# Four w_in blocks in whole float32, sums issued ahead, and powers by doubling in a one-core hybrid layer

## The chip, the cores and the metric

The kernel runs on one core of a Trainium2 chip. Its engines are TensorE (PE, and PEld for its weight loads), VectorE (DVE), ScalarE (ACT), GpSimd (POOL) and SyncE (SP, which issues most loads). The metric is device time of one execution in microseconds.

## The reference, cut to what matters

One layer of a hybrid block for 256 tokens of width 1024: a state space mixer and a sparse attention side by side, then a mixture of 32 experts.

```python
mod = cs @ ada_w[l] + ada_b[l]                      # cs = silu(c); six vectors of 1024
sh1, sc1, g1, sh2, sc2, g2 = jnp.split(mod[:, None, :], 6, axis=-1)
h = rms_norm(x, norm1_g[l]) * (1.0 + sc1) + sh1
proj = h @ w_in                                     # q, six k/v blocks, gates, u, merge gates
# s5_mixer(u): powers of ab = exp(lam * dt), complex, 64 states in each of 32 groups
mag = jnp.exp(lr * dt)
ab_re, ab_im = mag * jnp.cos(li * dt), mag * jnp.sin(li * dt)
bu = einsum(ug, bb); s = associative_scan(combine, (a, bu)); y = einsum(s, c) + d_skip * ug
# compress_kv: overlapping blocks of 32 keys (values), each through a small MLP
blocks = kv[:, idx] + pos[:, None, :]
return jax.nn.gelu(blocks @ w1) @ w2
...
merged = g_attn * (attn @ nsa_w_o) + g_ssm * (ssm @ ssm_w_o)
x = x + g1 * (merged @ w_out)
x = x + g2 * hier_moe(rms_norm(x, norm2_g[l]) * (1.0 + sc2) + sh2, ...)
```

## The kernel before, in words

Weights stream from HBM through rings of slots of 8 KB a partition (`room`, `load`, `set_rings`); a load waits until its slot's last reader is done. The first ring has five slots (`ringA`). Loads go out on SP's queue in order.

The first stage computes `mod`, h and the first four blocks of w_in: u0 and u1 (the mixer's input, 256 columns each), kc and vc (keys and values to be compressed). It runs over k = 0 to 7, 128 rows of the model width at a time. For each k:

- `mod_sum` multiplies `csb` (silu of c, repeated) with the part of ada_w for this k in eight float32 matmuls; TensorE packs four of them side by side. ScalarE copies the result to `msk`.
- `mod_end` transposes `msk` on TensorE; DVE reduces it and makes `modT` (shift) and `Gm` (gain).
- DVE makes `hf`, the row block of h, from the normalised and transposed input (`xnT`). ScalarE makes it again, rounded to float32r, as `hTh`; DVE subtracts for the rest, `hTl`.
- ScalarE rounds the slab of w_in for this k to float32r (`hi`, line 381), DVE subtracts for `lo` (line 382). `halves` hands out the two halves of the tiles `whi` and `wlo` in turn.
- `mm3` multiplies: high by high, high by low, low by high, three float32r matmuls of 256 columns each, eight times: 24 for a k.

Later projections (`proj_T`, `proj_N`) go the same way with `split` in place of the slab's halves, and read `hTh` and `hTl` of all k; the first of them is ks.

Beside it DVE and GpSimd prepare the mixer: exponent, sine and cosine of ab in small operations of 16 columns; `pows`, ab to the powers 2 to 4, and `pk4`, multiples of 4 up to 32, each from the one before by `cmul` with six operations; `sq`, two squarings more. GpSimd and DVE multiply B with the powers (`cmul2`), GpSimd C (`cmul`), and DVE copies the C powers to `Vc` (line 579). TensorE transposes the B powers to `Wt`. Then follow U (DVE transposes u), the matmuls x and pst, the projection ks, the compression of the keys (`blk`, `pc`, from line 706), and the scan on GpSimd and DVE. For each of four quarters n a tile `blk` is taken from a pair in turn; GpSimd zeroes its last column, DVE fills the rest.

The order on each engine isn't that of the source: a scheduler with its own estimates sets it when the program is built. Each engine takes its instructions in the order so set.

Of the kernel before, what the change touches and what calls it, by code (L numbers as in the profile page):

```python
# [52 lines left out]
def hybrid(ctx: ExitStack, tc: tile.TileContext, A, out, dbg=None, stop=None):  # L53
# [477 lines left out]
    for j in (2, 3, 4):  # L531
        cmul(V, pows[:, j, 0], pows[:, j, 1], pows[:, j - 1, 0], pows[:, j - 1, 1], pows[:, 1, 0], pows[:, 1, 1], u1, u2)
# [5 lines left out]
    for k in range(2, 9):  # L538
        cmul(V, pk4[:, k, 0], pk4[:, k, 1], pk4[:, k - 1, 0], pk4[:, k - 1, 1], pk4[:, 1, 0], pk4[:, 1, 1], u1, u2)
# [164 lines left out]
    for n in range(4):  # L704
# [4 lines left out]
        blk = cz.tile([128, 2, 4, 4, 16], F32, name=f"blk{n}", tag="blk", bufs=2)  # L709
        G.memset(blk[:, :, :, :, 15:16].rearrange("p k c g o -> p k c (g o)"), 0.0)  # L710
# [717 lines left out]
```

## Time and profile before

| | |
|---|---|
| time, median of 3 runs | 608.26 us (606.21 to 609.49) |
| profiled execution | 604.61 us, span 602.9 us |
| TensorE busy | 532.2 us (88%) |
| weight loads | 364.7 us (60%) |
| DVE busy | 351.0 us (58%) |
| ScalarE busy | 199.1 us (33%) |
| GpSimd busy | 203.2 us (34%) |
| HBM read | 166.30 MB, 278 GB/s over the span |

The shares are means over stages with different limits, so they are read by stage. A row of the timeline gives the start of the first of a run of equal instructions, how long they took together, how many there are, and in brackets the idle time before it with what ended it. Matmuls are pipelined: the distance of their starts tells their rate, not their length. TensorE's granted clock has two levels, 1.2 and 2.4 GHz; 1.00 in a row is the upper one.

### The profile page before, as it was taken

How to read it: one execution, taken by the hardware profiler on the slowest of the kernel's cores; microseconds unless marked ns; L12 is line 12 of the kernel's file. 1: busy time of each engine (PE TensorE's matmuls, PEld its weight loads, DVE VectorE, ACT ScalarE, POOL GpSimd, SP SyncE). 2: the span in 40 equal slices, each digit the busy share in tenths (PEclk: the TensorE clock that was granted, in tenths of full speed). 3: DMA queues.
4: the chain of work that ended last, by engine and by line, in shares of the span. 5: the costliest groups of instructions: out<-in, count | busy, mean ns of one | idle time of the engine just before them, and what ended most of it. 6: DMA issues, size and time to landing. Idle time of an engine off the chain costs nothing. (4 is left out here: it accounts for less than half of the span.)

```text
span 602.9 us, 10837 instructions
## 1 busy us (share of the span) xinstructions
PE 532.2 (88%) x4173; PEld 364.7 (60%) x4174; DVE 351.0 (58%) x942; ACT 199.1 (33%) x461; POOL 203.2 (34%) x299
## 2 busy tenths in 40 slices
PE   0769699879888999999989998999999989999983
PEld 0446597568888888888877997444434433333321
DVE  7999948999477867687866766422222221211213
ACT  3363446332244655554543444111111101010102
POOL 3079307587269544688977000000000000000000
PEclk9999899797998999999999999999999999999997
DMA  8774633967546323654499697977999999999992
GB/s 321 309 270 142 217 133 124 366 202 264 173 179 203 114 106 109 242 167 148 145 382 368 232 403 288 341 278 300 404 422 421 419 419 423 419 421 421 421 366 74
DMA packets 27867, 168.12 MB, mean 279 GB/s; under 512 B 3106, under 2 KB 3234, under 8 KB 10274
## 3 DMA queue, kind: packets, MB, share of 16 engines
q1 hardware_dynamic: 25506, 158.97, 68.4%
q0 software_dynamic: 2304, 8.39, 4.1%
q8 instruction: 35, 0.57, 0.4%
q14 instruction: 22, 0.18, 0.1%
HBM read 166.30 MB, written 1.05 MB: 278 GB/s over the span
## 5 line engine op out<-in xcount | busy, mean ns | idle before, releaser
L1345 POOL TENSOR_TENSOR x<-x,fg 128x512 f32<-128x512 f32 x1 | 1.3, 1269 | 266.4 <-DVE x L1347 266.4
L1188 PE MATMUL guq<-gu,room__4521 128*32 128x512 f32 (+1 forms) x512 | 85.8, 602 | 1.3 <-DMA gu<-in_egu_dram 1.3
L1161 PEld LDWEIGHTS pgq<-room__4521,x 128*128 128x128 f32 x288 | 38.1, 190 | 54.2 <-issue 15.8
L1165 DVE TENSOR_SCALAR room__4521<-pgq,Gm,modT 128x128 f32<-128x128 f32 x36 | 14.7, 409 | 85.0 <-PE pgq L1161 74.4
L1163 ACT ACTIVATE room__4521<-pgq,modT,Gm 128x128 f32<-128x128 f32 x36 | 16.5, 458 | 125.1 <-PE pgq L1161 125.1
L1161 PE MATMUL pgq<-room__4521,x 128*128 128x128 f32 x288 | 50.5, 298 | 7.7 <-DVE room__4521 L1165 4.5
L918 POOL TENSOR_SCALAR pr<-pr,st 128x128 f32<-128x128 f32 (+1 forms) x64 | 38.4, 618 | 26.5 <-DVE st L915 16.4
L353 POOL TENSOR_SCALAR adt<-adt,ct 128x256 f32<-128x256 f32 x64 | 35.4, 570 | 21.5 <-DMA adt<-in_adat_dram 21.4
L240 PE MATMUL pm<-ada,csb 128*32 128x256 f32 x256 | 21.6, 432 | 21.1 <-DVE csb L216 16.6
L1211 PE MATMUL dnq<-ed,acq 128*32 128x512 f32 (+1 forms) x224 | 38.9, 598 | 0.0
L1214 DVE SCALAR_TENSOR_TENSOR gb<-dnq,wsq,gb 128x512 f32<-128x512 f32 x18 | 13.5, 750 | 38.7 <-PE dnq L1211 38.7
L913 ACT ACTIVATE pr<-s,st 128x128 f32<-128x128 f32 (+1 forms) x64 | 26.2, 422 | 27.1 <-DVE st L909 26.3
L1220 PE MATMUL acc<-gb,room__4521 128*128 128x512 f32 x72 | 33.3, 605 | 0.0
L1188 PEld LDWEIGHTS guq<-gu,room__4521 128*32 128x32 f32 (+1 forms) x512 | 16.7, 112 | 24.8 <-issue 16.6
L1220 PEld LDWEIGHTS acc<-gb,room__4521 128*128 128x128 f32 x72 | 12.9, 189 | 20.4 <-issue 20.2
L240 PEld LDWEIGHTS pm<-ada,csb 128*32 128x32 f32 x256 | 7.7, 119 | 28.7 <-DVE csb L216 16.2
L354 POOL TENSOR_TENSOR adt<-adt 128x512 f32<-128x512 f32 x16 | 23.6, 1482 | 0.3
L290 PE MATMUL pj_gs<-hTh,wlo 128*128 128x256 f32 x64 | 19.3, 302 | 2.8 <-DVE wlo L281 2.8
L1211 PEld LDWEIGHTS dnq<-ed,acq 128*32 128x32 f32 (+1 forms) x224 | 9.5, 113 | 19.9 <-issue 17.7
L288 PE MATMUL p<-oTh,whi 128*128 128x256 f32 x64 | 18.4, 287 | 0.8 <-ACT whi L280 0.8
L289 PE MATMUL pj_gs<-hTl,whi 128*128 128x256 f32 x64 | 19.1, 298 | 0.0
L290 PE MATMUL p<-oTh,wlo 128*128 128x256 f32 x64 | 18.4, 288 | 0.6 <-DVE wlo L281 0.6
(558 smaller groups left out, 1600.6 us busy)
## 6 DMA issues: line engine op xcount, KB each, us to landing
gu<-in_egu_dram SPq DMA_DIRECT2D x64, 1024.0 KB, 17.4
ed<-in_edn_dram SPq DMA_DIRECT2D x28, 1024.0 KB, 16.1
ada<-in_adat_dram SPq DMA_DIRECT2D x16, 1024.0 KB, 6.6
adt<-in_adat_dram POOLq DMA_DIRECT2D x16, 512.0 KB, 5.2
slab<-in_w_dram SPq DMA_DIRECT2D x8, 512.0 KB, 8.8
cw<-in_cw_dram SPq DMA_DIRECT2D x4, 1024.0 KB, 4.9
win_q<-in_win_dram SPq DMA_DIRECT2D x4, 1024.0 KB, 4.7
win_gs<-in_win_dram SPq DMA_DIRECT2D x4, 1024.0 KB, 5.7
```

The costliest lines, as they stand in the source:

```text
L240: T.matmul(pm_k[32 * t:32 * t + 32, 0:256], lhsT=csb[:, 2 * t + j], rhs=slot[:, 2 * t + j], start=j == 0, stop=j == 1, tile_position=(0, 3 ...
L288: T.matmul(o, lhsT=ah, rhs=bh, start=start, stop=False)
L289: T.matmul(o, lhsT=ah, rhs=bl, start=False, stop=False)
L290: pe_last[0] = T.matmul(o, lhsT=al, rhs=bh, start=False, stop=stop)
L353: G.tensor_scalar(w[:, t], w[:, t], ct[:, 4 * h + t:4 * h + t + 1], 1.0, op0=ALU.mult, op1=ALU.mult)
L354: G.tensor_add(w[:, 0:2], w[:, 0:2], w[:, 2:4])
L913: S.activation(pr[:, a_:b_], src, AF.Exp, bias=st[:, 1, z:z + 1], scale=0.125, accum_out=st[:, 2, z:z + 1])
L918: G.tensor_scalar(pr[:, a_:b_], pr[:, a_:b_], st[:, 3, z:z + 1], 1.0, op0=ALU.mult, op1=ALU.mult)
L1161: T.matmul(pg[:, k % 4, 0:S_], lhsT=x[:, b, 128 * k:128 * k + 128], rhs=O[:, b, 0:S_], start=b == 0, stop=b == 1)
L1188: gl_ = T.matmul(gu[r], lhsT=xe[:, k, r], rhs=wgu(e, k), start=k == 0, stop=k == 7, tile_position=(0, s_ * e))
L1211: T.matmul(dn[r], lhsT=ac[:, c, r], rhs=wdn(e, c)[:, 512 * h:512 * h + 512], start=c == 0, stop=c == 1, tile_position=(0, s_ * e))
L1220: T.matmul(acc[b][h], lhsT=OT[0:M, sl], rhs=ty2[0:M, h], start=False, stop=last)
```

## The change

- The loop over k multiplies `hf` and the slab as they are, in float32; the slab's `hi` and `lo` are gone. `hTh` is a ScalarE copy of `hf`. A whole-float32 matmul is two instructions on TensorE.
- The sums of two k are issued ahead, and `rows` makes a block's `modT`, `Gm`, `hf` one k ahead of its matmuls; `hf` has three buffers.
- Two slots more for the first loads: the tiles `whi` and `wlo`, not used until ks now.
- The powers come by doubling: `times` multiplies several powers by one in four wider operations.
- ScalarE copies all C powers to `Vc`.
- The key blocks are two fixed tiles, whose last column DVE zeroes once.

```diff
     ada1, slab = [], []
+    set_rings([Late("whi"), Late("wlo")] + [ringA] * NA)
...
+    def rows(p_):
+        mod_end(*p_)
+        k = p_[3]
+        hf = pp.tile([128, 256], F32, name=f"hf{k}", tag="hf", bufs=3)
+        hfs.append(hf)
+        V.tensor_scalar(hf, xnT[:, k], Gm[:, 0, k:k + 1], modT[:, 0, k:k + 1], op0=ALU.mult, op1=ALU.add)
+        S.copy(hTh[:, k], hf)
+        V.tensor_sub(hTl[:, k], hf, f32(hTh[:, k]))
+    pms = [mod_sum(ada1[0], 0, 0, "s"), mod_sum(ada1[1], 0, 1, "s")]
+    rows(pms[0])
     for k in range(8):
-        mod_end(*mod_sum(ada1[k], 0, k, "s"))
-        hf = pp.tile([128, 256], F32, name=f"hf{k}", tag="hf", bufs=2)
...
-        hi, lo = halves()
-        S.copy(hi, slab[k])
-        V.tensor_sub(lo, slab[k], f32(hi))
+        if k < 6:
+            pms.append(mod_sum(ada1[k + 2], 0, k + 2, "s"))
+        if k < 7:
+            rows(pms[k + 1])
+        hf, w4 = hfs[k], slab[k]
         for i in range(2):
             for b in range(2):
-                mm3(o4[i][:, b], hTh[:, k, sl], hTl[:, k, sl], hi[:, c], lo[:, c], k + b == 0, k + b == 8)
+                T.matmul(o4[i][:, b], lhsT=hf[:, 128 * b:128 * b + 128], rhs=w4[:, 256 * i:256 * i + 256], start=k + b == 0, stop=k + b == 8)
...
-    for j in (2, 3, 4):
-        cmul(V, pows[:, j, 0], pows[:, j, 1], pows[:, j - 1, 0], pows[:, j - 1, 1], pows[:, 1, 0], pows[:, 1, 1], u1, u2)
+    def times(o, a, b):
+        n = b.shape[1]
+        p1, p2 = pwt[:, 0, 0:n], pwt[:, 1, 0:n]
+        for p_, r in ((p1, 0), (p2, 1)):
+            V.tensor_tensor(p_, a[:, r].unsqueeze(1).unsqueeze(2).to_broadcast([128, n, 2, 16]), b, op=ALU.mult)
+        V.tensor_sub(o[:, :, 0], p1[:, :, 0], p2[:, :, 1])
+        V.tensor_add(o[:, :, 1], p1[:, :, 1], p2[:, :, 0])
+    times(pows[:, 2:3], pows[:, 1], pows[:, 1:2])
+    times(pows[:, 3:5], pows[:, 2], pows[:, 1:3])
...
-    for k in range(2, 9):
-        cmul(V, pk4[:, k, 0], pk4[:, k, 1], pk4[:, k - 1, 0], pk4[:, k - 1, 1], pk4[:, 1, 0], pk4[:, 1, 1], u1, u2)
+    for n in (1, 2, 4):
+        times(pk4[:, n + 1:2 * n + 1], pk4[:, n], pk4[:, 1:n + 1])
...
-                if j == 0:
-                    S.activation(dst, ccur[r][ps_], AF.Copy, scale=-1.0 if r else 1.0)
-                else:
-                    V.tensor_scalar(dst, ccur[r][ps_], -1.0 if r else 1.0, None, op0=ALU.mult)
+                S.activation(dst, ccur[r][ps_], AF.Copy, scale=-1.0 if r else 1.0)
...
+    blks = [cz.tile([128, 2, 4, 4, 16], F32, name=f"blk{n}") for n in range(2)]
+    for blk in blks:
+        V.memset(blk[:, :, :, :, 15:16].rearrange("p k c g o -> p (k c g o)"), 0.0)
...
-        G.memset(blk[:, :, :, :, 15:16].rearrange("p k c g o -> p k c (g o)"), 0.0)
+        blk = blks[n % 2]
```

The order of the built program shows the moves at three places.

TensorE, from its first sum to its first block. `pm` is the bank of a sum, `msk` its copy, `ph` the transposed xn, `hf` the float32 row block, `hTh` its float32r part. Before:

```order
L240 MATMUL pm_238<-ada_0_85,csb 32x256 x8
L248 MATMUL pm_238<-ident,msk_247 128x128 x2
L229 MATMUL ph_188<-ident,scr 128x128 x4
L229 MATMUL ph_194<-ident,scr 128x128 x4
L229 MATMUL ph_214<-ident,scr 128x128 x4
L229 MATMUL ph_220<-ident,scr 128x128 x4
L288 MATMUL pj_u_234<-whi,hTh 128x256
```

With the change:

```order
L241 MATMUL pm_238<-ada_0_85,csb 32x256 x8
L241 MATMUL pm_249<-ada_1_89,csb 32x256 x8
L249 MATMUL pm_238<-ident,msk_247 128x128 x2
L230 MATMUL ph_188<-ident,scr 128x128 x4
L230 MATMUL ph_194<-ident,scr 128x128 x4
L241 MATMUL pm_270<-ada_2_93,csb 32x256 x8
L249 MATMUL pm_249<-ident,msk_258 128x128 x2
L230 MATMUL ph_214<-ident,scr 128x128 x4
L230 MATMUL ph_220<-ident,scr 128x128 x4
L249 MATMUL pm_270<-ident,msk_279 128x128 x2
L398 MATMUL pj_u_234<-slab_87,hf_266 128x256 x2
```

The sums of k=1 and 2 and their transposes of msk now stand ahead of the first block, whose operands are `hf` and the slab itself.

DVE, between `hf` of k=2 and `hf` of k=3 (here its end). `mr`, `modT`, `Gm` belong to k=3, `pwt`, `pk`, `pwA`, `pwB` to the powers, `scr`, `b` to the B powers. Before, at the same step (`hf` of k=2 is `hf_349`, of k=3 `hf_396`):

```order
L377 TENSOR_SCALAR hf_349<-scr,Gm,modT 128x256
L475 TENSOR_TENSOR u_688<-pows 128x16
L476 TENSOR_TENSOR u_689<-pows 128x16
L251 TENSOR_TENSOR modT<-mr_392,pk 128x2
L467 TENSOR_TENSOR scr<-pows,b_710 128x256
L468 TENSOR_TENSOR scr<-pows,b_709 128x256
L477 TENSOR_TENSOR pows<-u_688,u_689 128x16
L252 SCALAR_TENSOR_TENSOR Gm<-modT,pk 128x1
...
L377 TENSOR_SCALAR hf_396<-scr,Gm,modT 128x256
```

With the change (`hf_345` is that of k=3):

```order
L479 TENSOR_TENSOR scr<-pows,b_565 128x256
L549 TENSOR_TENSOR pwt<-pk_671 128x128
L252 TENSOR_TENSOR modT<-mr_341,pk 128x2
L480 TENSOR_TENSOR b_568<-scr 128x256
L550 TENSOR_TENSOR pk_671<-pwt 128x4x16
L551 TENSOR_TENSOR pk_671<-pwt 128x4x16
L253 SCALAR_TENSOR_TENSOR Gm<-modT,pk 128x1
L478 TENSOR_TENSOR scr<-pows,b_568 128x256
L563 COPY pwA<-pk_671 128x8x16 x2
L564 TENSOR_SCALAR pwB<-pk_671 128x8x16
L383 TENSOR_SCALAR hf_345<-scr,Gm,modT 128x256
```

Before, `hf` of k=3 follows that of k=2 after 11 rows; now nearly all powers stand between the two.

DVE at the last block (k=7). `hf_584` and `hf_450` are its row block before and now; `wlo<-win_ks` are the two low halves of the weights of the next projection. Before:

```order
L377 TENSOR_SCALAR hf_584<-scr,Gm,modT 128x256
L477 TENSOR_TENSOR pk_824<-u_688,u_689 128x16
L379 TENSOR_TENSOR hTl<-hf_584,hTh 128x256
L550 TENSOR_SCALAR aS<-pk_824 128x16
L551 COPY aS<-pk_824 128x16
L472 TENSOR_TENSOR u_688<-pk_824 128x16
...
L551 COPY aS<-sq_887 128x16
L393 STREAM_TRANSPOSE scr<-pj_u_234 128x256 x2
L281 TENSOR_TENSOR wlo<-win_ks,whi 128x1024
L393 STREAM_TRANSPOSE scr<-pj_u_235 128x256 x2
L281 TENSOR_TENSOR wlo<-win_ks,whi 128x1024
```

With the change:

```order
L385 TENSOR_TENSOR hTl<-hf_403,hTh 128x256
L385 TENSOR_TENSOR hTl<-hf_432,hTh 128x256
L282 TENSOR_TENSOR wlo<-win_ks,whi 128x1024
L251 TENSOR_REDUCE mr_446<-pm_415 128x2
L282 TENSOR_TENSOR wlo<-win_ks,whi 128x1024
L252 TENSOR_TENSOR modT<-mr_446,pk 128x2
L253 SCALAR_TENSOR_TENSOR Gm<-modT,pk 128x1
L383 TENSOR_SCALAR hf_450<-scr,Gm,modT 128x256
L385 TENSOR_TENSOR hTl<-hf_450,hTh 128x256
L404 STREAM_TRANSPOSE scr<-pj_u_234 128x256 x2
L404 STREAM_TRANSPOSE scr<-pj_u_235 128x256 x2
```

The two low halves of ks moved from behind the last row block and the transposes of U to in front of them.

## Rows read from the trace of the kernel before

**Rows 1.** Busy time by stretch: us, busy us (instructions) by engine, clock, DMA.
```profile
23.00:81.00 58.00, 45.99 (x357) 35.31 (x355) 56.15 (x206) 26.48 (x53) 31.45 (x38) 0.94 0.56 203
...
30.00:45.00 15.00, 10.25 (x92) 7.56 (x95) 14.86 (x49) 10.09 (x24) 11.50 (x13) 0.93 0.78 274
```
**Rows 2.** Waits, 23 to 81 us: total us, times, longest.
```profile
ACT hTh L378 <- DVE Gm L252: 13.2, 4, 10.2
```
**Rows 3.** DVE's timeline: start, us, engine, line, operation, count [idle before].
```profile
12.46 1.23 DVE L382 TENSOR_TENSOR wlo<-slab,whi 128x1024 fp32r<-128x1024 f32 x1 [0.46 <-ACT whi L381]
...
18.27 1.22 DVE L382 TENSOR_TENSOR wlo<-slab,whi 128x1024 fp32r<-128x1024 f32 x1
...
26.83 0.17 DVE L440 TENSOR_SCALAR r__629<-r__629 128x16 f32<-128x16 f32 x1
...
29.85 0.17 DVE L461 TENSOR_TENSOR pows<-mag,cs__633 128x16 f32<-128x16 f32 x1
```
**Rows 4.** TensorE's timeline, start of the stage, same columns.
```profile
16.57 1.93 PE L240 MATMUL pm<-ada,csb 128*32 128x256 f32 x16 [16.57 <-DVE csb L216]
...
20.49 3.87 PE L229 MATMUL ph<-ident,scr 128*128 128x128 f32 x16 [0.75 <-DVE scr L225]
...
25.48 0.58 PE L288 MATMUL pj_u<-whi,hTh 128*128 128x256 f32 x1 [1.12 <-ACT hTh L378]
...
26.63 3.21 PE L240 MATMUL pm<-ada,csb 128*32 128x256 f32 x26
```
**Rows 5.** TensorE's timeline, end of the stage.
```profile
80.70 0.28 PE L289 MATMUL pj_vc<-hTl,whi 128*128 128x256 f32 x1
...
80.82 0.28 PE L290 MATMUL pj_vc<-hTh,wlo 128*128 128x256 f32 x1
...
92.64 0.39 PE L288 MATMUL pj_ks<-hTh,whi 128*128 128x256 f32 x1
```
**Rows 6.** TensorE's timeline, whole-float32 matmuls of 512 columns in the last third.
```profile
431.41 3.70 PE L1220 MATMUL acc<-gb,room__4521 128*128 128x512 f32 x8
...
434.95 0.61 PE L1161 MATMUL pgq<-room__4521,x 128*128 128x128 f32 x4
```
**Rows 7.** DVE's groups, 23 to 80 us (two rows) and 30 to 66: count | busy, mean ns.
```profile
L382 DVE TENSOR_TENSOR wlo<-slab,whi 128x1024 fp32r<-128x1024 f32 x6 | 8.3, 1379 | 0.0
...
L579 DVE TENSOR_SCALAR Vc<-b 64x256 f32<-64x256 f32 x16 | 6.7, 420 | 0.1
...
L472 DVE TENSOR_TENSOR u<-pk 128x16 f32<-128x16 f32 x4 | 2.1, 522 | 0.1
```
**Rows 8.** DVE's timeline, a small product late in the stage.
```profile
76.64 0.17 DVE L472 TENSOR_TENSOR u<-pk 128x16 f32<-128x16 f32 x1
```
**Rows 9.** GpSimd's timeline, the last product of the powers.
```profile
65.32 0.72 POOL L477 TENSOR_TENSOR b<-gw 128x256 f32<-128x256 f32 x1 [0.59 <-DVE Vc L579]
```
**Rows 10.** TensorE's timeline, 61 to 69 us.
```profile
61.90 1.07 PE L240 MATMUL pm<-ada,csb 128*32 128x256 f32 x16 [1.91 <-DVE mr L250]
...
66.14 0.39 PE L288 MATMUL pj_u<-whi,hTh 128*128 128x256 f32 x1 [2.15 <-ACT hTh L378]
...
67.97 0.42 PE L288 MATMUL pj_u<-whi,hTh 128*128 128x256 f32 x1
...
68.18 0.42 PE L289 MATMUL pj_u<-wlo,hTh 128*128 128x256 f32 x1
```
**Rows 11.** Loads before 110 us: size, median us to landing.
```profile
cw<-in_cw_dram SPq DMA_DIRECT2D x4, 1024.0 KB, 4.9
...
win_ks<-in_win_dram SPq DMA_DIRECT2D x1, 1024.0 KB, 7.0
...
pk<-in_pk_dram SPq DMA_DIRECT2D x1, 360.0 KB, 12.3
```
**Rows 12.** TensorE's timeline, the wait on the key blocks.
```profile
108.24 1.09 PE L717 MATMUL pc<-cw,blk 128*64 128x256 f32 x2 [2.21 <-POOL scr L628]
```
**Rows 13.** Memory traffic by slice of a fortieth of the span (page).
```profile
GB/s 321 309 270 142 217 133 124 366 202 264 173 179 203 114 106 109 242 167 148 145 382 368 232 403 288 341 278 300 404 422 421 419 419 423 419 421 421 421 366 74
```

More of the change, by code (lines that the diff above doesn't have):

```diff
@@ L373, in hybrid @@
     o4 += [bank(f"pj_{nm}", tag).rearrange("p (m t) -> p m t", m=2) for nm, tag in (("kc", "o"), ("vc", "s"))]
-    for k in range(8):
-        mod_end(*mod_sum(ada1[k], 0, k, "s"))
-        hf = pp.tile([128, 256], F32, name=f"hf{k}", tag="hf", bufs=2)
-        V.tensor_scalar(hf, xnT[:, k], Gm[:, 0, k:k + 1], modT[:, 0, k:k + 1], op0=ALU.mult, op1=ALU.add)
-        S.activation(hTh[:, k], xnT[:, k], AF.Identity, bias=modT[:, 0, k:k + 1], scale=Gm[:, 0, k:k + 1])
-        V.tensor_sub(hTl[:, k], hf, f32(hTh[:, k]))
-        hi, lo = halves()
-        S.copy(hi, slab[k])
-        V.tensor_sub(lo, slab[k], f32(hi))
+    hfs = []
+    def rows(p_):
[8 more added lines that the diff above has]
+    rows(pms[0])
+    for k in range(8):
+        if k < 6:
[3 more added lines that the diff above has]
+        hf, w4 = hfs[k], slab[k]
         for i in range(2):
             for b in range(2):
-                sl, c = slice(128 * b, 128 * b + 128), slice(256 * i, 256 * i + 256)
-                mm3(o4[i][:, b], hTh[:, k, sl], hTl[:, k, sl], hi[:, c], lo[:, c], k + b == 0, k + b == 8)
+                T.matmul(o4[i][:, b], lhsT=hf[:, 128 * b:128 * b + 128], rhs=w4[:, 256 * i:256 * i + 256], start=k + b == 0, stop=k + b == 8)
         for i in range(2, 4):
             for m in range(2):
-                c = slice(256 * i + 128 * m, 256 * i + 128 * m + 128)
-                mm3(o4[i][:, m], hi[:, c], lo[:, c], hTh[:, k], hTl[:, k], k + m == 0, k + m == 8)
+                pe_last[0] = T.matmul(o4[i][:, m], lhsT=w4[:, 256 * i + 128 * m:256 * i + 128 * m + 128], rhs=hf, start=k + m == 0, stop=k + m == 8)
     for i in range(2):
@@ L530, in hybrid @@
         S.copy(Wt[:, 2 * gq:2 * gq + 2].rearrange("p a b c -> p (a b) c"), pst)
-    for j in (2, 3, 4):
-        cmul(V, pows[:, j, 0], pows[:, j, 1], pows[:, j - 1, 0], pows[:, j - 1, 1], pows[:, 1, 0], pows[:, 1, 1], u1, u2)
+    pwt = pp.tile([128, 2, 4, 2, 16], F32, name="pwt")
+    def times(o, a, b):
[7 more added lines that the diff above has]
+    times(pows[:, 3:5], pows[:, 2], pows[:, 1:3])
     pk4 = pp.tile([128, 9, 2, 16], F32, name="pk4")
@@ L547, in hybrid @@
             sq, sq_ = pp.tile([128, 2, 16], F32, name=f"sq{i_}"), sq
-            cmul(V, sq[:, 0], sq[:, 1], sq_[:, 0], sq_[:, 1], sq_[:, 0], sq_[:, 1], u1, u2)
+            times(sq.unsqueeze(1), sq_, sq_.unsqueeze(1))
         V.tensor_copy(aS[:, i_, 0], sq[:, 0:1].to_broadcast([128, 2, 16]))
@@ L708, in hybrid @@
         tick(f"cw{n}")
-        blk = cz.tile([128, 2, 4, 4, 16], F32, name=f"blk{n}", tag="blk", bufs=2)
-        G.memset(blk[:, :, :, :, 15:16].rearrange("p k c g o -> p k c (g o)"), 0.0)
+        blk = blks[n % 2]
         for kd in range(2):
```

## The prediction

> **What bounds the kernel now.** I read the page's slices first, then busy time by stretch, the waits of the first stage, and the timelines of its engines. The change touches the stage from 23 to 81 us, in which eight steps k each make one row block of h and multiply it with one slab of w_in. There DVE is busy 56.15 of 58 us, TensorE 45.99 and the DMA engines 56% [rows 1]. The longest wait is ScalarE's for Gm, 13.2 us, and what it waits for stands on DVE [rows 2]. So DVE's queue bounds this stage: TensorE's first block starts at 25.48 [rows 4], its last ends near 81.1 [rows 5], and every engine's later work stands behind that. Behind the scan the instruction order is the same in both kernels but for a few swaps, so I price the first stage and then ask whether its shift reaches the end.
>
> **Start.** Two lo halves leave DVE's queue ahead of the first block, at 12.46 and 18.27, 1.2 us each; the first also has 0.46 us of waiting in front. So the first sum, which csb releases at 16.57 [rows 4], moves to about 14.9 [rows 3]. But the new TensorE order puts three sums and three pairs of msk transposes ahead of the first block, where one of each stood. A sum takes 1.93 us at TensorE's lower clock and 1.07 at the upper, the 16 transposes of xn 3.87 [rows 4, 10]. In this trace TensorE still runs at the lower level at 26.63 (26 instructions in 3.21 us, 0.12 each; at the upper level 0.067), though the transposes from 20.49 ran without a gap [rows 4]. I therefore take the lower level: 14.9, three sums 5.8, 22 transposes at 3.87 / 16 = 0.24 each 5.3, and about 1.5 for the last msk copy, reduction and hf: first block at 27.5. At the upper level from the second sum on it would be 24.0. So this edit costs 2.0 or gives 1.5; I take +2.0.
>
> **Matmuls.** A float32r matmul of 256 columns starts 0.12 us after the last one [rows 5]; a block has 24, 2.9 us. A whole-float32 matmul is two instructions; the one with 512 columns shows 8 in 3.54 us to the next start, 0.44 each [rows 6], so 256 columns take half of that, about 0.215 (a little less than 0.22, for the last start also changes the work). A block has 16 of them, 3.4 us; eight blocks, 27.5 against 23.0. TensorE's own work grows by 4.5 us, and this is paid wherever it isn't waiting.
>
> **DVE.** Gone in the stretch are six more lo halves (8.3 us) and sixteen copies of C powers (6.7 us) [rows 7]. These go to ScalarE, which loses eight hi copies for them and was 26.48 of 58 us busy [rows 1], so it is no bound. 72 small operations for the powers become 28. What is left between hf of k=2 and hf of k=3 decides, for the order puts the sines, all powers up to the eighth and half of the B powers in between. From 30 to 45 us DVE ran 49 instructions in 15 us [rows 1]; without the one lo half of 1.2 us that is 0.29 each, with 16 operations of 256 columns among them. The new stretch has fewer of these, 7 in 44; I use 0.27. Hf of k=0 is ready at 27.4, ten instructions later hf of k=2 and its low part at 30.1; the sines take 3.0, as from 26.83 to 29.85 [rows 3]: 33.1. Then come 44 instructions, the last of them hf of k=3: 33.1 + 44 x 0.27 = 45.0. 25 more end with hf of k=4: 51.8.
> The rate is slow because GpSimd works at the same time: a 128x16 product takes 0.522 us on the mean between 30 and 66 [rows 7] and 0.17 after GpSimd's last product at 65.32 [rows 8, 9]. The Trainium skill, "GPSIMD Engine Reference", section 1, says that GpSimd's SBUF interfaces are shared with VectorE and contend with instructions that have two SBUF inputs. The trace agrees (0.522 against 0.17), and the new products have two such inputs; by this rule they stay slow, and without it the 44 would take 44 x 0.17 = 7.5 us instead of 11.9.
>
> **The walk.** Block 0 from 27.5, half of it still at the lower level: to 32.9. Block 1 with sum 3: 37.4. Sum 4 and transposes, block 2: 42.2. TensorE waits 2.8 for hf; block 3 from 45.0 to 48.4; waits 3.4; block 4 from 51.8 to 55.2. Then eight Wt transposes 1.0, sums 5 and 6 2.1, eight Wt transposes 1.0, msk transposes 0.6, 2.1 for hf 5 (it covers sum 7 and eight more Wt transposes), blocks 5 and 6 7.1, Wt transposes 1.0, block 7 3.4: 73.5, against 81.1. The U transposes on DVE no longer have a ks half between them: -0.4. The stage is 8.0 us shorter.
>
> **The other edits.** The two slots let loads 3 and 4 go out at once instead of at 18.56, but the DMA engines are full until 25 us in any case: nothing by itself. The key blocks' zeroing leaves GpSimd's queue, where one wait of TensorE, 2.2 us, ended on it [rows 12]; DVE's scan fills that time too, so 0 to -1.5, taken as 0. The ks load goes out after sum 6 (58.3 in the walk), and its two lo halves stand ahead of the last hf on DVE: about 0.6 to issue, 4.9 to land as the cw loads do [rows 11], a hi and two lo halves at 1.2 each, 0.7 to hf: 68.1. TensorE wants it at 70.1, so 2 us of cover.
> Whether the shift lasts: loads of the later stages go out when slots come free, so they move with the compute, and the memory traffic of the last third, flat near 420 GB/s [rows 13], starts earlier by as much. I carry all of it over. Sum: -8.0. The profiled run took 604.6 us (span 602.9 and 1.7 around it), so 596.6; it lay 3.7 under the median of 608.3. Against the median: **600.3**.
>
> **Rivals.**
> 1. DVE is not late. With the upper clock from the start (-3.4) and DVE at 0.17 us per instruction, hf 3 is there when TensorE comes: 24.0 + three blocks, two sums = 36.7, then two blocks 43.5 plus little, and the 18.3 from block 4's end on. The stage ends at 63 to 69: -12 to -18, middle 594. For it: fewer large DVE operations stand beside GpSimd than before. Against: the rows above on GpSimd and on the clock.
> 2. The ks load stands in front of the last block. If it lands as late as the 360 KB of pk did, 12.3 us [rows 11], hf 7 comes 7.4 - 2.0 = 5.4 us after TensorE wants it: -2.6, 605.7. For it: DVE and ScalarE take work strictly in their order. Against: pk went out into full queues; here three loads at most are under way, and its own row in the kernel before is 7.0.
> 3. Slower: TensorE at its lower level through the float32 block. Each of the 128 instructions then costs 0.43. After waits of 1.91 and 2.15 us the trace shows spacings of 0.21 for float32r at 67.97, so a wait can bring it [rows 10]; the new order has two waits of about 3 us. The Trainium skill, "TensorE: Matmul & The Clock Gate", section "Why this matters for your kernels", also asks for no idle gaps between bursts, for the clock falls back behind them; the row agrees. About 6 us of loss hide in the waits for DVE, so the change turns slower from some 75 of the 128 at the lower level on; at 100 of them it is 100 x 0.215 - 6 - 8.0 - 2 (block 0's share, counted above) = +5, 613. Against: float32 ran at the upper level at 431 [rows 6], and from 23 to 81 the mean granted clock was 0.94 [rows 1].
> 4. The front moves and the end doesn't, because a later load or semaphore holds its time: 608. Against: no load waits for anything but slots and data.
>
> **Chances.** Forecast, DVE late at k=3 and 4: 0.55, its own range 596 to 604.5. Rival 1: 0.18. Rival 2: 0.10. Rival 3: 0.09. Rival 4: 0.08. A measurement of this kernel can tell about 0.5%, 3.0 us. Faster by more than that (under 605.2): 0.51 of the first, all of rival 1, 0.04 of rival 2, 0.73. Within: 0.04, 0.05 and 0.08 from the first, second and fourth, 0.17. Slower: rival 3 and 0.01 of rival 2, 0.10. The range of 8 in 10 reaches from the low end of rival 1 to a little past rival 2's: 590 to 607.
>
> **What would show it.** Right: TensorE waits on hf in blocks 3 and 4 and hardly elsewhere; float32 spacing of 0.21; the first block near 27.5; U's transposes end near 74; ks starts near 84 instead of 92.64; later rows the same, about 8 us earlier. Wrong: no wait at block 3 (rival 1); a wait of the last hf on the ks load (rival 2); spacings of 0.43 in most float32 blocks (rival 3); an early ks and an unmoved end (rival 4).

## The result

The changed kernel takes 599.3 us (median of 4 runs, 598.49 to 600.24); the kernel before took 607.36 in the same comparison (606.21 to 609.49). The ratio is 0.9853, 95% interval 0.9808 to 0.9898: 1.5% faster. 600.3 was predicted. The profiled execution took 599.78 us, span 598.1, against a span of 602.9 before.

Leads tell the story. A lead is the start of a row in the trace of before minus the start of the same row after. The first matmul of ks started at 92.64 [rows 5] and starts at 80.36: 12.3 us, where 8 were predicted. At the end 4.8 are left between these two executions; the medians are 8.1 apart, for the profiled execution of before was 2.8 under its median and that of the changed kernel 0.5 above its own.

Busy time by stretch, changed kernel, columns as in [rows 1]:

```profile
23.00:81.00 58.00, 53.34 (x415) 43.11 (x416) 35.46 (x138) 30.15 (x70) 29.34 (x42) 0.94 0.58 221
...
30.00:45.00 15.00, 11.17 (x55) 8.56 (x55) 15.00 (x53) 7.62 (x20) 10.24 (x14) 0.82 0.75 307
...
40.80:47.00 6.20, 6.19 (x16) 5.04 (x17) 6.20 (x26) 3.46 (x10) 4.18 (x6) 0.55 0.07 28
```

In the stage of [rows 1] DVE went from 56.15 to 35.46 us and TensorE from 45.99 to 53.34: DVE no longer bounds the whole stage. From 30 to 45 us it still does: it is busy all 15, in 53 instructions where there were 49. TensorE's clock is 0.82 there, and 0.55 from 40.8 to 47, a stretch almost wholly at the lower of its two levels.

TensorE's timeline, changed kernel (start, us, engine, line, operation, count, idle time before):

```profile
14.77 3.64 PE L241 MATMUL pm<-ada,csb 128*32 128x256 f32 x32 [14.77 <-DVE csb L217]
...
19.91 1.07 PE L241 MATMUL pm<-ada,csb 128*32 128x256 f32 x16
...
21.19 1.04 PE L230 MATMUL ph<-ident,scr 128*128 128x128 f32 x8
...
23.60 1.97 PE L398 MATMUL pj_u<-slab,hf 128*128 128x256 f32 x8 [1.16 <-issue]
...
40.81 3.78 PE L398 MATMUL pj_u<-slab,hf 128*128 128x256 f32 x8 [3.83 <-DVE hf L383]
...
44.38 1.91 PE L401 MATMUL pj_kc<-hf,slab 128*128 128x256 f32 x4
...
47.09 1.89 PE L398 MATMUL pj_u<-slab,hf 128*128 128x256 f32 x8
...
69.05 0.64 PE L610 MATMUL pst<-Vc,B 128*32 128x128 f32 x16
...
80.36 0.38 PE L289 MATMUL pj_ks<-hTh,whi 128*128 128x256 f32 x1
```

The rows answer to [rows 4, 5]. The first block starts at 23.60 (25.48 before). The one long wait is 3.83 us for hf of k=3. Behind it the same float32 instruction, two to a matmul, costs twice as much: eight took 3.57 us from 40.81 to 44.38; the eight at 47.09 have 1.89 in their row for 3.78. The work behind the blocks starts at 69.05, where it started at 81.03.

DVE's timeline, changed kernel: the first power, hf of k=3 and k=4, the reductions for k=5 and 6.

```profile
28.28 0.17 DVE L473 TENSOR_TENSOR pows<-mag,sn 128x16 f32<-128x16 f32 x1
...
40.36 0.40 DVE L383 TENSOR_SCALAR hf<-scr,Gm,modT 128x256 f32<-128x256 f32 x1
...
46.19 0.59 DVE L383 TENSOR_SCALAR hf<-scr,Gm,modT 128x256 f32<-128x256 f32 x1
...
54.80 0.39 DVE L251 TENSOR_REDUCE mr<-pm 128x2 f32<-128x8 f32 x2 [6.92 <-PE pm L249]
```

From the start of the first power to that of hf of k=3 it is 12.1 us; 6.92 us idle follow only behind hf of k=4, where DVE waits for TensorE's sums.

Where did the lead go? It is 12.3 us at ks, 11.5 near 237 us, 7.3 near 279, 6.9 at the router near 350, 6.4 at the last accumulation. The loss lies between 250 and 280. First the kernel before there (GpSimd, SyncE, TensorE):

```profile
263.40 0.57 POOL L351 DMA_DIRECT2D adt<-in_adat_dram  x1 [0.30 <-POOL agr L359]
...
266.88 3.76 POOL L353 TENSOR_SCALAR adt<-adt,ct 128x256 f32<-128x256 f32 x8
...
265.86 20.29 SPq L94 DMA_DIRECT2D nwo<-in_nwo_dram  x3
...
275.63 0.33 PE L923 MATMUL pta<-ident,pr 128*128 128x128 f32 x1 [0.66 <-POOL pr L918]
```

The changed kernel, same views:

```profile
251.68 0.57 POOL L352 DMA_DIRECT2D adt<-in_adat_dram  x1 [0.30 <-DVE st L936]
...
260.79 2.80 POOL L354 TENSOR_SCALAR adt<-adt,ct 128x256 f32<-128x256 f32 x4 [4.83 <-DMA adt<-in_adat_dram]
...
252.58 25.68 SPq L94 DMA_DIRECT2D nwo<-in_nwo_dram  x3
...
266.44 0.47 PE L944 MATMUL pta<-ident,pr 128*128 128x128 f32 x1 [3.81 <-POOL pr L939]
```

GpSimd loads parts of ada_w in half loads (`adt`), multiplies them, and between two such pieces scales attention weights (`pr`) that TensorE transposes. Before, SyncE's megabytes of `nwo` were issued 2.5 us behind the half load of 263.40, which landed 5.3 us after its issue and kept nobody waiting. Now they are issued 0.9 us behind that of 251.68, which takes 9.0 us to land; GpSimd starts on it at 260.79, after 4.83 us of waiting. The scaling stands behind it, TensorE waits 3.81 us and then works at the lower clock until about 271.4 (granted clock 0.50; float32r every 0.21 us).

### The profile page after: what moved, and what is told of

The parts are those of the page before. It is cut to its first block, busy times and chain, and to the rows that moved or that the text cites. A ratio compares the mean times of both kernels' runs of the same rounds, so it can differ in the third digit from the quotient of the medians.

```text
span 598.1 us, 10630 instructions
## 1 busy us (share of the span) xinstructions
PE 532.3 (89%) x4109; PEld 366.3 (61%) x4110; DVE 317.2 (53%) x876; ACT 196.6 (33%) x469; POOL 198.3 (33%) x295
## 5 line engine op out<-in xcount | busy, mean ns | idle before, releaser
L1209 PE MATMUL guq<-gu,room__4330 128*32 128x512 f32 (+1 forms) x512 | 84.0, 602 | 1.1 <-DMA gu<-in_egu_dram 1.1
L939 POOL TENSOR_SCALAR pr<-pr,st 128x128 f32<-128x128 f32 (+1 forms) x64 | 35.0, 562 | 24.4 <-DVE st L936 14.2
L241 PE MATMUL pm<-ada,csb 128*32 128x256 f32 x256 | 18.2, 415 | 14.8 <-DVE csb L217 14.8
L398 PE MATMUL pj_u<-slab,hf 128*128 128x256 f32 x64 | 17.7, 419 | 5.2 <-DVE hf L383 4.1
L944 PE MATMUL pta<-ident,pr 128*128 128x128 f32 x64 | 15.6, 296 | 6.0 <-POOL pr L939 6.0
L291 PE MATMUL pj_ga<-hTh,wlo 128*128 128x256 f32 x64 | 19.8, 309 | 0.0
## 6 DMA issues: line engine op xcount, KB each, us to landing
slab<-in_w_dram SPq DMA_DIRECT2D x8, 512.0 KB, 12.5
```

Source lines behind the costliest of these rows:

```text
L241: T.matmul(pm_k[32 * t:32 * t + 32, 0:256], lhsT=csb[:, 2 * t + j], rhs=slot[:, 2 * t + j], start=j == 0, stop=j == 1, tile_position=(0, 3 ...
L291: pe_last[0] = T.matmul(o, lhsT=al, rhs=bh, start=False, stop=stop)
L398: T.matmul(o4[i][:, b], lhsT=hf[:, 128 * b:128 * b + 128], rhs=w4[:, 256 * i:256 * i + 256], start=k + b == 0, stop=k + b == 8)
L939: G.tensor_scalar(pr[:, a_:b_], pr[:, a_:b_], st[:, 3, z:z + 1], 1.0, op0=ALU.mult, op1=ALU.mult)
L1209: gl_ = T.matmul(gu[r], lhsT=xe[:, k, r], rhs=wgu(e, k), start=k == 0, stop=k == 7, tile_position=(0, s_ * e))
```

## The experiments

Leads in us over the profiled execution of the kernel before, each worked out as above (before: 92.64, 146.30, 318.61, 354.97 and 589.03), and the ratio to the kernel before in each comparison. Gates is the first matmul of the gates (`og`), last head group the last `po`, router the first `plg`, last sum the last accumulation (`acc`):

| kernel | ks | gates | last head group | router | last sum | ratio (95%) |
|---|---|---|---|---|---|---|
| changed | 12.3 | 11.6 | 7.0 | 6.9 | 6.4 | 0.9853 (0.9808 to 0.9898) |
| one_sum | 3.6 | 2.6 | 2.3 | 2.4 | 2.5 | 0.9915 (0.9873 to 0.9957) |
| old_powers | 4.8 | 4.5 | 4.9 | 5.4 | -0.2 | 0.9943 (0.9897 to 0.9989) |
| f32r_blocks | 11.5 | 11.3 | 12.1 | 12.6 | 10.0 | 0.9838 (0.9757 to 0.9919) |
| c_powers_on_dve | 12.7 | 12.2 | 3.8 | 4.3 | 2.5 | 0.9806 (0.9724 to 0.9888) |
| small_parts_undone | 11.3 | 10.3 | 4.2 | 4.6 | 3.5 | 0.9805 (0.9715 to 0.9895) |
| powers_late | 10.2 | 9.4 | 8.2 | 8.6 | 5.5 | 0.9865 (0.9803 to 0.9926) |
| powers_and_ks_late | 11.9 | 10.9 | 7.7 | 7.7 | 7.8 | 0.9802 (0.9741 to 0.9862) |
| scale_on_dve | 12.4 | 12.2 | 7.7 | 6.7 | 3.9 | 0.9854 (0.9797 to 0.9911) |
| loads_of_nwo_later | 12.4 | 11.1 | 7.3 | 7.4 | 6.3 | 0.9874 (0.9822 to 0.9925) |
| scale_groups_3_4_on_dve | 12.7 | 12.5 | 14.4 | 14.2 | 11.7 | 0.9783 (0.9693 to 0.9873) |
| scale_groups_3_4_again | 12.3 | 11.9 | 10.9 | 12.4 | 11.2 | 0.9725 (0.9688 to 0.9762) |

The leads are of one execution each and the ratios of several, so a single lead at the end need not match its ratio. The parts don't add up: without the sums ahead ks loses 8.7 of the 12.3 us, without the doubling 7.5.

### What in the first stage pays

**one_sum**: the sums not ahead.

```diff
-    pms = [mod_sum(ada1[0], 0, 0, "s"), mod_sum(ada1[1], 0, 1, "s")]
-    rows(pms[0])
     for k in range(8):
...
-            rows(pms[k + 1])
+        rows(mod_sum(ada1[k], 0, k, "s"))
```

Expected: 

> The changed kernel with each k's sum and row block issued in its own step again, not ahead. Theory A (TensorE's clock rises after the first sum, so sums ahead cost little, and DVE's queue from hf 2 to hf 4 sets the stage): the first block starts 1 to 2 us earlier, hf 3 and hf 4 stand some 90 rows behind the first hf on DVE as before and come near 45; the last block ends near 71, time +1 to +3 us against the changed kernel. Rival (the chain sum, copy, transposes, reduction, hf is what the issue ahead hides, 2 to 3 us for each k): the last block ends 8 us or more later, and the time is that of the kernel before or near it, 605.

```profile
18.72 3.89 PE L230 MATMUL ph<-ident,scr 128*128 128x128 f32 x16
...
22.55 0.41 DVE L383 TENSOR_SCALAR hf<-scr,Gm,modT 128x256 f32<-128x256 f32 x1
...
31.80 0.17 DVE L251 TENSOR_REDUCE mr<-pm 128x2 f32<-128x8 f32 x1 [3.30 <-ACT msk L243]
...
34.53 0.40 DVE L383 TENSOR_SCALAR hf<-scr,Gm,modT 128x256 f32<-128x256 f32 x1
...
49.39 3.78 PE L393 MATMUL pj_u<-slab,hf 128*128 128x256 f32 x8 [6.79 <-DVE hf L383]
```

The rival's size held: ks starts at 89.09, 8.7 us later than in the changed kernel. hf of k=0 is ready at 23.0, but hf of k=1 only at 34.9: DVE is done with the sines and the first two powers by 28.5, stands idle 3.30 us for the sum of k=1, which comes behind block 0, and takes more powers before hf. The rest of the powers stands ahead of hf of k=3, and TensorE waits 6.79 us for that, ahead of 49.39. So the chain of a k shows once, with 3.3 us; the larger part is what DVE's order puts in front of hf of k=3.

**old_powers**: the powers by `cmul` as before, one from the other.

```diff
-    times(pows[:, 2:3], pows[:, 1], pows[:, 1:2])
...
+    for k in range(2, 9):
+        cmul(V, pk4[:, k, 0], pk4[:, k, 1], pk4[:, k - 1, 0], pk4[:, k - 1, 1], pk4[:, 1, 0], pk4[:, 1, 1], u1, u2)
```

Expected: 

> The changed kernel with the powers multiplied one from the other again, 72 operations of 16 columns in place of 28 wider ones. In the order hf 3 stands 54 rows behind hf 2 (62 now), since the longer chain falls behind it. Theory A (only what stands ahead of hf 3 and hf 4 counts; DVE idles 6.9 us behind that): hf 3 no later, the rest of the chain fills DVE's idle time; last block within 1.5 us of 69, time 0 to +1.5 us. Rival (DVE's total work decides: 44 more operations of 0.17 to 0.29 us, 7.5 to 13 us): last block 5 us later or more, time +4 us or more.

```profile
61.59 0.16 DVE L251 TENSOR_REDUCE mr<-pm 128x2 f32<-128x8 f32 x1
...
61.80 1.94 PE L241 MATMUL pm<-ada,csb 128*32 128x256 f32 x16 [8.61 <-DVE mr L251]
```

My theory fell. hf of k=3 came earlier, as said (38.7), but the longer chain ran to 61.59 ahead of the reductions for k=5 and 6, so TensorE waited 8.61 us there; ks starts at 87.81, 7.5 us later. The 44 operations more cost this because DVE's order has them in front of the reductions; c_powers_on_dve below adds 6.7 us to DVE and costs nothing.

**f32r_blocks**: the blocks as `mm3` with hi and lo halves, without the two slots.

```diff
-        hf, w4 = hfs[k], slab[k]
+        hi, lo = halves()
+        S.copy(hi, slab[k])
+        V.tensor_sub(lo, slab[k], f32(hi))
```

Expected: 

> The changed kernel with the four blocks as three float32r matmuls again, hi halves on ScalarE, lo halves on DVE, and without the two extra slots (they lie in the halves' tiles). Theory A (what counts on DVE is what stands ahead of hf 3 and hf 4; three lo halves stand there, 3.7 us, and a block is 0.5 us shorter on TensorE): the last block ends 1 to 3 us later, time +1 to +3 us. Rival (the eight lo halves, 10 us of DVE, are the whole gain): +7 us or more, near 606.

```profile
65.63 0.28 PE L290 MATMUL pj_vc<-hTh,wlo 128*128 128x256 f32 x1
...
67.51 1.15 PE L543 MATMUL pst<-ident,bw 128*128 128x128 f32 x8 [1.60 <-ACT Wt L544]
```

Neither held as written. The last block's last matmul starts at 65.63, so the blocks end some 3 us earlier than in the changed kernel; but sixteen Wt transposes now come behind it and wait 1.60 us for ScalarE, and ks starts at 81.17, 0.8 us later. The whole-float32 blocks, undone alone, gain or lose nothing that these runs can tell. That TensorE pays in its own time what DVE saves on the lo halves fits this, but the new order of the Wt transposes came with the edit and isn't told apart from it.

**c_powers_on_dve**: the branch `if j == 0` in front of the copies of C powers is put back.

Expected: 

> The changed kernel with the sixteen copies of C powers on DVE again: 6.7 us of DVE work, by the order eight of them behind hf of k=4, the rest between hf of k=6 and the transposes of U. Theory A (eight fall in the 6.92 us that DVE idles ahead of the reductions for k=5 and 6, the rest ahead of and behind hf 7): ks starts 0 to 2 us later, time 0 to +2. Rival (DVE's total work sets the stage, as the old powers showed, +7.4 us at ks for their 44 operations): ks starts 5 us later or more, time +4 or more.

```profile
51.76 0.92 DVE L601 TENSOR_SCALAR Vc<-b 64x256 f32<-64x256 f32 x2 [1.33 <-POOL b L485]
```

ks starts at 79.94, 0.4 us earlier than in the changed kernel, as A had it: the copies fill DVE's gap behind hf of k=4 (between them DVE even waits 1.33 us for GpSimd). This move by itself is worth nothing at ks.

**small_parts_undone**: no `Late` slots, the key blocks zeroed by GpSimd.

```diff
-    set_rings([Late("whi"), Late("wlo")] + [ringA] * NA)
...
+        G.memset(blk[:, :, :, :, 15:16].rearrange("p k c g o -> p k c (g o)"), 0.0)
```

Expected: 

> The changed kernel without the two extra slots for the first loads, and with the key blocks' last columns zeroed by GpSimd again. Prediction's view (the DMA queues are full until 25 us in any case, and DVE's scan fills the time of the key blocks' wait): ks starts within 1 us of 80.36, time within 1.5 us of the changed kernel. Rival (the sums ahead need the loads ahead): sum 3 or 4 waits for its load at 28 to 32 us, and ks starts 2 us later or more.

```profile
40.97 3.64 PE L240 MATMUL pm<-ada,csb 128*32 128x256 f32 x32 [2.15 <-DVE mr L250]
```

ks is 1.0 us later, at 81.39, and the ratio isn't higher than the changed kernel's. The reason expected of the rival (a sum that waits for its load) isn't in the trace: at 40.97 a sum waits 2.15 us for a reduction on DVE. The two parts are worth 1 us in the stage at most.

### What still bounds it

**powers_late**: the multiples of 4 and all that follows from them inside `with tc.issue_after(hf_i[5].ins)`, which queues them on DVE behind hf of k=5.

Expected: 

> The multiples of 4 (pk4, pwA, pwB, aS, sq) stand behind hf of k=5 on DVE; all else is the changed kernel. In its trace TensorE idles 3.83 us ahead of block 3, at 36.98 to 40.81, and then runs 16 float32 instructions and more at 0.43 instead of 0.215 (block 3 takes 6.3 us instead of 3.4). Theory A (that wait is DVE's queue between hf 2 and hf 3, and the lower clock follows from the wait): hf 3 comes about 4 us earlier, the wait goes below 0.5 us, block 3 takes 3.4 us, the last block ends near 62 instead of 69, and ks starts near 73.5. Theory B (the lower clock comes at about 40 us whatever TensorE did before): the wait goes, the low stretch stays, the last block ends near 65. For the end: if the front's shift is carried, 592 (A) or 595 (B); if the stage near 260 us takes it back, 598 to 599.

```profile
37.94 1.99 PE L398 MATMUL pj_u<-slab,hf 128*128 128x256 f32 x8 [0.87 <-DVE hf L383]
...
42.21 1.99 PE L398 MATMUL pj_u<-slab,hf 128*128 128x256 f32 x8 [0.56 <-DVE hf L383]
...
65.92 3.58 PE L398 MATMUL pj_u<-slab,hf 128*128 128x256 f32 x8 [4.03 <-DVE hf L383]
...
57.37 1.99 ACT L281 CAST whi<-win_ks 128x1024 fp32r<-128x1024 f32 x2 [0.17 <-PE pj_vc L401]
...
62.71 1.23 DVE L282 TENSOR_TENSOR wlo<-win_ks,whi 128x1024 fp32r<-128x1024 f32 x1
```

Half of A held. The waits at blocks 3 and 4 fell to 0.87 and 0.56 us, and with them the slow stretch: 1.99 us for eight instructions at both, where it was 3.78. So the lower clock in that place follows from the wait (B falls); in one_sum, with 6.79 us of waiting ahead of 49.39, it came back (3.78 us for eight). But block 7 then waits 4.03 us, and ks starts at 82.46, 2.1 us later. I read this as the ks load being late. It wasn't: ScalarE rounded ks at 57.37, and the lo halves start at 62.71, behind the powers.

**powers_and_ks_late**: the powers behind hf of k=4 and, in `split`, the lo halves of ks behind hf of k=7.

```diff
-            (G if (nm, i) in POOL_LO else V).tensor_sub(lv, s, f32(hv))
+            with tc.issue_after(hf_i[7].ins) if nm == "ks" else nullcontext():
+                (G if (nm, i) in POOL_LO else V).tensor_sub(lv, s, f32(hv))
```

Expected: 

> The multiples of 4 behind hf of k=4 on DVE, and the two lo halves of ks behind hf of k=7; else the changed kernel. In powers_late TensorE's waits at blocks 3 and 4 fell to 0.87 and 0.56 us, all float32 instructions there ran at 0.215, and then block 7 waited 4.03 us for hf 7, which stood behind the lo halves, whose load hadn't landed. Theory A (that order alone held block 7): no wait over 1 us behind block 4; the last block ends near 64 (block 4's end near 45.7 and the 18.3 that follow it), ks starts near 75.5, 5 us ahead of the changed kernel's. Rival (the ks load, or the powers now ahead of hf 5 and 6, are late all the same, as the reductions were in old_powers): a wait of 3 us or more comes back, and ks starts at 79 or later. The end: 594 if the 5 us are carried, 599 if the wait near 260 us takes them.

```profile
53.75 1.94 PE L241 MATMUL pm<-ada,csb 128*32 128x256 f32 x16 [2.48 <-DVE mr L251]
...
48.61 0.16 DVE L574 TENSOR_SCALAR aS<-pk 128x16 f32<-128x16 f32 x1
...
48.69 0.60 DVE L575 COPY aS<-pk 128x16 f32<-128x16 f32 x1
```

The same kernel, busy time of that stretch, columns as in [rows 1]:

```profile
41.10:53.60 12.50, 8.97 (x72) 6.50 (x72) 12.26 (x37) 8.08 (x19) 11.64 (x18) 0.96 0.52 174
```

The rival held in the main: ks starts at 80.77, though the wait is 2.48 us and not 3 or more. It moved to the reductions for k=5 and 6, ahead of 53.75. From 41.1 to 53.6 DVE is busy 12.26 us for 37 instructions; a TENSOR_SCALAR and a COPY, both of 128x16, cost 0.16 and 0.60 right behind each other.

**late_powers_without_gpsimd_c**: the same without GpSimd's products for C.

```diff
-            cmul(G, nxt[0], nxt[1], bc(pows[:, 1, 0]), bc(pows[:, 1, 1]), ccur[0], ccur[1], g1, g2)
-            ccur = nxt
+            pass
```

Expected: 

> powers_and_ks_late without GpSimd's products for the C powers (C itself is copied in their place, so later numbers differ, and its experts too; only the stage to ks is read). There the 29 operations for the multiples of 4 behind hf of k=4 took 12.4 us (41.14 to 53.55, 0.43 each; the same 128x16 copy 0.16 or 0.60) while GpSimd was busy 11.74 of 12.6 us. Theory A (GpSimd's instructions hold DVE's): the same 29 take 5 to 6.5 us, near 0.2 each, the reductions for k=5 and 6 come when the sums are ready, TensorE's wait of 2.48 us goes, and ks starts at 75 to 77 instead of 80.77. Rival (the small operations cost that by themselves, one waiting for the result of the other): 10 us or more, and ks stays near 80.

```profile
44.20:49.60 5.40, 5.24 (x40) 4.36 (x44) 5.22 (x38) 3.06 (x7) 0.42 (x1) 1.00 0.52 193
```

And its timelines of DVE and TensorE:

```profile
47.91 0.17 DVE L575 COPY aS<-pk 128x16 f32<-128x16 f32 x1
...
52.16 0.39 DVE L251 TENSOR_REDUCE mr<-pm 128x2 f32<-128x8 f32 x2 [2.53 <-PE pm L249]
...
77.02 0.39 PE L290 MATMUL pj_ks<-hTh,whi 128*128 128x256 f32 x1
```

Theory A held. With GpSimd nearly idle (0.42 of 5.4 us, 11.64 of 12.5 in the run above) DVE does 38 instructions in 5.22 us, 0.14 each instead of 0.33, and the same copy costs 0.17. The reductions come when their sums do (DVE waits 2.53 us for TensorE at 52.16), and ks starts at 77.02, 3.8 us earlier. So GpSimd's instructions are what makes DVE's slow here. The products for C have to be made somewhere; no order of theirs was tried.

### Where the lead is lost

**scale_on_dve** and **scale_groups_3_4_on_dve**: one scaling of attention weights on DVE, and then, with `qc > 1` for `nm == "211"`, all eight of groups 3 and 4.

```diff
-                    G.tensor_scalar(pr[:, a_:b_], pr[:, a_:b_], st[:, 3, z:z + 1], 1.0, op0=ALU.mult, op1=ALU.mult)
+                    (V if nm == "211" else G).tensor_scalar(pr[:, a_:b_], pr[:, a_:b_], st[:, 3, z:z + 1], 1.0, op0=ALU.mult, op1=ALU.mult)
```

Expected of the first: 

> The changed kernel with one of the sixteen scalings of the attention weights by their sums (the fourth of the third group of heads) on DVE instead of GpSimd. There GpSimd waited 4.83 us for a load (260.79), TensorE 3.81 us for the scaling behind it (266.44), and then ran at half clock to 271.7; the lead on the kernel before fell from 12.35 to 7.33 us. Theory A (the lead is lost in that one wait and its clock): TensorE's wait goes below 1 us, the lead past 275 us stays 11 to 12.5, and the end comes 4 to 5 us earlier: 595. Rival (a later scaling or load takes the wait's place, or the lower clock comes anyhow): lead 7 to 9 by 330 us, time 598 to 600.

```profile
280.80 0.47 PE L944 MATMUL pta<-ident,pr 128*128 128x128 f32 x1 [6.80 <-POOL pr L939]
```

The rival held: the wait went on to the next scaling on GpSimd, 6.80 us long, and the lead was 6.7 us at the router.

Expected of the second: 

> The changed kernel with the eight scalings of groups 3 and 4 of the attention weights on DVE, so that TensorE waits for no GpSimd instruction behind its load of adt. With one of them moved, TensorE's wait went from 266.44 (3.81 us) to the next group's first scaling at 280.80 (6.80 us). Theory A (GpSimd's queue takes the lead, in whichever scaling stands behind a late load): no wait over 1.5 us on a scaling between 255 and 320 us, lead 10 us or more at 330 us, time 595 to 596. Rival (DVE, with some 4 us more work there, becomes the bound, or the lead is lost to something else): lead 7 or less at 330 us, time 599 or more.

No wait of TensorE on a scaling is left between 255 and 320 us, and the lead there is 14.4 us. This is theory A. But the edit did two things: GpSimd, free of the scalings, issued its half load at 245.88, 7.5 us ahead of nwo, so here the two didn't meet at all, and the run doesn't part this from TensorE's being off GpSimd's queue.

**loads_of_nwo_later**: ScalarE issues the loads of nwo, behind a copy (`pt_211`) near 266 us.

```diff
+    with tc.issue_after(pt_211.ins):
+        for m in range(3):
+            S.dma_start(nwo[m], A["nwo"][m])
```

Expected: 

> The changed kernel with the three loads of nwo issued by ScalarE, two right behind its copy of the weights of the last head of group 3 and the third a little later, and not by SyncE when their slots come free. In the changed kernel SyncE issues the first at 252.58, 0.9 us behind GpSimd's second half load of adt (251.68), which then lands at 260.8, 9.1 us after its issue; in the kernel before it came 2.5 us behind (263.40 and 265.86), and the half load was there after 3.5 us. Theory A (the megabytes of nwo beside it make the half load late, GpSimd waits 4.83 us for it, TensorE 3.81 for GpSimd): GpSimd's wait near 258 falls below 1.5 us, TensorE's ahead of that head's transposes below 1.5 us, and the lead on the kernel before stays 10.5 us or more to 290 us; time 595 to 596. Rival (GpSimd's own queue of loads and multiplications is too slow whatever lands): TensorE's wait stays above 2.5 us, the lead falls to 7 or 8; time 599.

```profile
256.33 3.77 POOL L354 TENSOR_SCALAR adt<-adt,ct 128x256 f32<-128x256 f32 x8
...
275.75 1.84 POOL L354 TENSOR_SCALAR adt<-adt,ct 128x256 f32<-128x256 f32 x4 [5.51 <-DMA adt<-in_adat_dram]
...
266.83 0.86 ACTq L988 DMA_DIRECT2D nwo<-in_nwo_dram  x2
...
280.14 0.33 PE L944 MATMUL pta<-ident,pr 128*128 128x128 f32 x1 [2.89 <-POOL pr L939]
```

Both were right in part. At 256.33 GpSimd takes its half load without a wait and multiplies eight pieces at a stretch; TensorE doesn't wait there and the lead was still 10.6 us at 282 (A). But the megabytes issued at 266.83 then meet the next half loads, which take 8.0 and 7.3 us to land where the one before took 5.1: GpSimd waits 5.51 us ahead of 275.75, TensorE 2.89 ahead of 280.14, and 7.3 us of lead are left. So the collision is the cause, and moving it saves nothing.

The other kernels' traces say the same. In c_powers_on_dve, small_parts_undone, powers_late and powers_and_ks_late nwo is issued 0.9 us behind that half load too, which takes 8.5 to 8.8 us to land; between the rows that before has at 237.02 and 284.44 they lose 2.6 to 4.3 us of lead, the changed kernel 4.2. In f32r_blocks it is issued 1.8 us behind, the half load lands after 6.2 us, GpSimd waits 0.76 us for it, and 1.6 us are lost:

```profile
252.79 0.57 POOL L351 DMA_DIRECT2D adt<-in_adat_dram  x1 [0.30 <-DVE st L939]
...
254.57 22.93 SPq L94 DMA_DIRECT2D nwo<-in_nwo_dram  x3
...
259.05 2.91 POOL L353 TENSOR_SCALAR adt<-adt,ct 128x256 f32<-128x256 f32 x4 [0.76 <-DMA adt<-in_adat_dram]
```

In late_powers_without_gpsimd_c it is 1.8 us behind too (6.1 us to land), and the loss is below 0.1 us. So about 1 us between two issues decides over some 2 to 4 us of lead. What else moves the leads from there to the last head group was not followed.

**scale_groups_3_4_again**: the kernel of scale_groups_3_4_on_dve in more runs.

Expected: 

> The kernel of scale_groups_3_4_on_dve once more, in more rounds. Theory A (TensorE off GpSimd's queue keeps the stage's lead of 12 us to the end, 4 to 5 us more than the changed kernel keeps): a ratio to the kernel before of 0.976 to 0.981, below the changed kernel's 0.9853. Rival (the first ratio of 0.9783 came from a few good runs): 0.983 or more.

592.02 us against 608.78, a ratio of 0.9725, still lower than theory A had it, and the interval of 0.9688 to 0.9762 lies below that of the changed kernel: with the eight scalings on DVE the kernel beats both.

## Why the prediction was right

The time was right, 600.3 for 599.3, and DVE as the bound up to k=4 too. But two terms were wrong by 4 and 5 us, with opposite signs, so that the total came out within 1 us is luck.

- **Start: the step that failed in the stage.** I took the lower clock for all three sums and 22 transposes, +2.0 us. The trace has the slow spacing in the first two sums, 32 instructions from 14.77 in 3.64 us; the third sum's 16 took 1.07, eight transposes 1.04, so the 22 transposes took some 3.1 us where 5.3 were forecast and the third sum 1.0 where 1.9 were. (The clock column reads 1.00 from 14.77 to 18.34 as well, so this level is read from the spacing alone.) The row of slow transposes was read in another order: in one_sum, where one sum stands ahead of them again and TensorE idles 1.28 us behind it, the 16 take 3.89 us as before. The first block came at 23.60, so the term was -1.9, and hf of k=0 to 2 came about 4 us earlier than forecast. The text's other figure, 24.0, is close by chance: it had the second sum at the upper level.
- **DVE.** 44 instructions at 0.27, 11.9 us, were forecast; from the first power's start to that of hf of k=3 it was 12.1, for 45 instructions. That GpSimd's work makes them slow was weighed from [rows 7 to 9] and is shown by late_powers_without_gpsimd_c. The rule of the Trainium skill ("GPSIMD Engine Reference", section 1: shared SBUF interfaces) agrees: 0.33 and 0.14 each. One of the slow ones is a COPY with a single input, though (0.60 against 0.17), so two inputs are not all that it takes here.
- **The walk.** Block 3 at 40.81 for 45.0, the shift of the start. Its wait was 3.83 for 2.8. I had no lower clock there; it came and doubled block 3, to 6.28 us. That covered the wait of 3.4 forecast at block 4, which never showed. Rival 3 was thus right about the mechanism and wrong about its reach: one block, not a hundred instructions (by its own terms a hundred cost 5.5 us, not 5). From block 4's end to the end of the stage I had 18.3; 18.5 were measured (50.55 to 69.05).
- **Whole float32.** +4.5 us on TensorE against 8.3 on DVE: f32r_blocks puts the sum of both near nothing at ks.
- **The other edits.** The slots and the key blocks at 0: together they are worth 1.0 us at ks by small_parts_undone. TensorE's wait for the key blocks didn't stay at 2.2 us: it is now 5.4 for DVE, and costs 1.7 us of the lead between ks and kw, the projection behind the key blocks; 1.0 us of it is back at the gates. The ks load had its cover: block 7 waited 0.23 us.
- **"I carry all of it over": the step that failed behind the stage.** 12.3 us at ks were 6.9 from the router on, for GpSimd's half load met the loads of nwo. Rival 4 had the kind of cause (a load that holds its time) but not the place or the size; its "against", that loads wait for slots and data alone, missed that loads of two queues meet: loads_of_nwo_later moved them, and the wait moved with them. Most of the loss hangs on whether 0.9 or 1.8 us lie between two issues, so another kernel can miss most of it, as f32r_blocks did. The Trainium skill ("DMA: Bandwidth & Descriptors", section "Issuing engines are not separate DMA queues") says that DMAs run on the same 16 engines and interleave whoever starts them; these runs agree, whether SyncE or ScalarE issued nwo (9.0 and 8.0 us to land, waits of 4.83 and 5.51 us on GpSimd's half load).
- **Behind the last accumulation** the profiled pair loses 1.5 us more: from 589.03 and 582.68 to the ends of the spans it is 13.9 us before and 15.4 after. Among the other kernels both lengths occur (13.7 to 13.9 and 15.4 to 15.6); what decides isn't settled.

## What to carry to other kernels

Price an edit on a busy queue by what stands behind it: the powers were moved twice, and each time the next row block or reduction was late instead. Look for the engine beside the bound as well as the bound: GpSimd slowed DVE here, and its load held TensorE 170 us later. And follow the lead, row by row, to the end: a stage that gains 12 us may hand 5 back where two queues' loads now meet, and the cheapest gain of this study, eight scalings moved to another engine, lay there.

## What was not expected of the hardware

The same kernel (that of scale_groups_3_4_on_dve), twice and on two chips, in the stretch from 364 to 371 us, columns as in [rows 1]. The first execution:

```profile
364.00:371.00 7.00, 6.50 (x20) 2.64 (x18) 2.10 (x17) 0.67 (x2) 0.00 (x0) 0.51 0.96 405
```

The second:

```profile
364.00:371.00 7.00, 5.39 (x31) 2.87 (x33) 3.27 (x24) 1.26 (x5) 0.00 (x0) 1.00 0.93 344
```

In one the clock was 0.51 and TensorE did 20 matmuls in 6.50 us, in the other 1.00 and 31 in 5.39. Short waits of TensorE on the router's results lie ahead in all kernels (0.5 to 1.0 us each in the changed one, from 364 to 372); the slow stretch follows them in some executions only. The lead falls from 14.2 to 11.4 us there in the first and stays at 12.4 in the second. Much of the spread of a kernel's runs may be such stretches; which executions get them was not found out. The Trainium skill ("TensorE: Matmul & The Clock Gate", Part 1) calls the number of slow matmuls at a kernel's start variable from run to run; this pair shows the like in the middle of one.
